# One-layer hybrid decoder step on one core: two-operand work of the FFN moved from GpSimd to VectorE

## The chip, the core and the metric

The kernel runs on one core of one Trainium2 chip. The metric is device time in microseconds (us) of one execution. Engines are named as the profile names them: PE is TensorE's matmul row and PEld its weight loads, DVE is VectorE, ACT is ScalarE, POOL is GpSimd, SP is SyncE, which here issues all large DMAs.

## The reference

The reference computes one decoder layer for 512 prompt tokens and 8 x 8 sample tokens (576 token columns in the kernel). What matters here is its second half, the output projection, the ConvGLU and the last norm:

```python
x = x + jnp.concatenate([ya, yb, yc], axis=-1) @ w_out        # 2048 x 2048
h2 = rms_norm(x, norm2)
gc, new_ffn = causal_dwconv(h2 @ w_gate, ffn_buf, ffn_conv_w) # 2048 x 5504, 3 taps
x = x + (jax.nn.silu(gc) * (h2 @ w_up)) @ w_down              # 5504 x 2048
y = rms_norm(x, final_norm)
```

All data is float32.

## The kernel before

Activations lie transposed, channels on the 128 partitions and 576 token columns along the free side, split into two halves of 288 columns (`HALF`). A float32 product is made of three matmuls in a reduced float32 form: every operand is split into a high part (ACT, a copy with rounding) and a low part (DVE, source minus high part). For weights that is `split_w` (lines 827 and 828), for activations `split_sb` (lines 174 and 175).

The program is written as one straight line. A scheduler puts the instructions in order for each engine, and each engine then works its list strictly in that order; an instruction waits on semaphores for its inputs and for buffers. The stages of the profiled execution are: input projection and attention (to about 970 us), output projection (`project(w_out, ...)`, to about 1155), a first change of stage (to about 1200) in which the second norm is prepared, gate and up products (to about 2160), a second change of stage (to about 2240), down products in four chunks (to about 2690), and a tail.

Gate, up and down use one level of Strassen's method in Winograd's form, `strassen` (line 839 is its matmul). One call loads four weight tiles b11, b12, b22, b21, forms combinations of them in place, splits seven tiles, and runs seven products. Each product is 24 matmuls of 128 x 288 in gate and up (8 blocks of 128 rows, three matmuls each, weight tiles 128 x 1024) and 15 in down (5 blocks, tiles 128 x 640). The products run into three PSUM tiles, `a`, `b` and `e`, in the order p1, p5, u2, p2, u3, p53, c21. Several products add into the same PSUM tile, so an eviction has to be read before the next product on that tile starts: u2 is read out of `a` before the product of u3 adds to it, u3 before that of c21. Between the two there is always one product on another tile.

Gate and up calls alternate: a gate call makes two gate tiles (`combine` with `gate_first` and `gate_second`, which multiply by the norm's factor `rstd2`), then an up call finishes the pair before it (`times`). The convolution and the activation of a gate pair (`conv_silu`: ACT, four DVE operations of 592 columns, ACT, two POOL multiplications) are put into the up call that follows it, one step after each eviction.

In the first change of stage, `own_halves` and `mixed_halves` split the last activations, and the rows `ssb` of sums of squares become `rstd2` (`rsqrt`: DVE line 184, ACT line 185, then DVE again). In the down stage `first_halves` prepares the activations of chunk 0 and `act_halves` those of chunks 1 to 3, during the chunk before, as far as the 28 slots for activations go; a chunk has 18. `add_to` adds each product to two of the 16 residual tiles.

The four weight combinations of one call are in lines 870 (DVE), 874 (POOL), 875 (DVE) and 880 (POOL).

Of the kernel before, what the change touches and what calls it, by code (L numbers as in the profile page):

```python
# [10 lines left out]
F32 = mybir.dt.float32  # L11
# [69 lines left out]
def decoder_step(ctx: ExitStack, tc, I, O):  # L81
# [778 lines left out]
    def strassen(load, X, evac, split, n, early=None):  # L860
# [13 lines left out]
        nc.gpsimd.tensor_sub(b12, b22, b12)  # L874
# [29 lines left out]
    for m in range(KD):  # L904
# [16 lines left out]
        else:  # L921
# [6 lines left out]
            nc.gpsimd.tensor_add(s12[:, :HALF], v0[:, HALF:], v[:, HALF:])  # L928
            nc.gpsimd.tensor_sub(s12[:, HALF:], s12[:, :HALF], v0[:, :HALF])
# [69 lines left out]
    def combine(sink0, sink1, sink2, sink3):  # L999
# [3 lines left out]
        def evac(place, ps):  # L1003
# [9 lines left out]
            elif place == "u3":  # L1013
                nc.scalar.copy(s2[:, HALF:], ps)
                nc.gpsimd.tensor_add(s1[:, HALF:], s2[:, HALF:], s1[:, HALF:])
# [10 lines left out]
    def gate_first(e, eng):  # L1026
        return lambda src: eng.tensor_mul(e[:, 2:2 + HALF], src, r0)

    def gate_second(e, eng):
        def sink(src):  # L1030
            eng.tensor_mul(e[:, 2 + HALF:2 + NP], src[:, :NPH], r1[:, :NPH])
            eng.tensor_mul(ext_a(e)[:, :, 2:10], src[:, NPH:].rearrange("p (b t) -> p b t", b=NB),
                           r1[:, NPH:].rearrange("p (b t) -> p b t", b=NB))
        return sink

    def conv_silu(ff, e, nst, f, nf):
# [55 lines left out]
    for nf in GROUPS:  # L1092
# [287 lines left out]
```

## Time and profile before

| | |
|---|---|
| median of 3 runs | 2761.15 us (2757.96 to 2763.15) |
| the profiled execution's own time | 2761.27 us |
| its span in the profile | 2759.5 us |
| PE busy | 2582.1 us (94% of the span) |
| PEld busy | 2514.7 us (91%) |
| DVE busy | 1952.0 us (71%) |
| POOL busy | 1273.4 us (46%) |
| ACT busy | 981.0 us (36%) |
| mean granted TensorE clock | 0.972 of full speed |

Matmuls are pipelined and their ends are modelled, so PE counts as busy while matmuls follow one another, and PE's work in a stretch is best read from the number of matmuls in it. An instruction that is held up while it runs shows as a longer duration, not as idle time. Idle time ahead of an instruction stands in brackets in a timeline, with the instruction that ended it. Line numbers are those of the kernel before; the changed kernel is 11 lines shorter, so its later lines have numbers smaller by 1 to 11.

### The profile page before, as it was taken

The numbers are of one execution on the slowest core, as the hardware profiler recorded it, in microseconds if no ns is written. First come the engines' busy times: TensorE is split into PE (matmuls) and PEld (weight loads), VectorE is DVE, ScalarE is ACT, GpSimd is POOL, SyncE is SP. The second block draws the span as 40 slices with busy tenths as digits, with TensorE's granted clock in tenths as the row PEclk, the third lists the DMA queues.
The fourth block names the chain that finished last, engine by engine and source line by source line (L and its number), as shares of the span: only waits on it lengthen the run. The fifth ranks groups of instructions, "written<-read, shape, count | busy, mean of one in ns | idle before, by whom it ended". The sixth has DMA issues, their size and how long they took to land.

```text
span 2759.5 us, 48907 instructions
## 1 busy us (share of the span) xinstructions
PE 2582.1 (94%) x19844; PEld 2514.7 (91%) x19844; DVE 1952.0 (71%) x2231; ACT 981.0 (36%) x1498; POOL 1273.4 (46%) x932
## 2 busy tenths in 40 slices
PE   8998998997988999889999999999999798989997
PEld 8988998997988999889999999999999698989997
DVE  5236467467477633597878788888878889898985
ACT  6121221221211333344444444444444444443445
POOL 0027027125248011465656555665656645454544
PEclk9999999999999999989999999999999899999999
DMA  8345368268466775335555555545555745444534
GB/s 254 112 105 146 88 178 216 73 174 218 124 172 170 240 243 184 123 102 161 163 159 158 165 157 155 166 155 163 160 158 166 251 150 153 147 147 146 158 101 143
DMA packets 602804, 441.60 MB, mean 160 GB/s; under 512 B 22167, under 2 KB 568642, under 8 KB 596178
## 3 DMA queue, kind: packets, MB, share of 16 engines
q1 hardware_dynamic: 602578, 438.47, 53.4%
q8 instruction: 156, 2.56, 0.4%
q14 instruction: 70, 0.57, 0.1%
HBM read 398.17 MB, written 127.50 MB: 190 GB/s over the span
## 4 chain that ended last, share of the span: by engine, by line
PE 50%; DVE 19%; issue 11%; DMA 8%; POOL 5%; ACT 4%; SPq 2%; ACTq 0%; DVEq 0%; POOLq 0%
PE acc L839 16%; PE acc L155 6%; PE acc L156 6%; PE acc L157 6%; DVE wl L828 5%; PE pt L839 4%; PE s L839 4%; PE ps L839 4%; ACT wh L827 4%; DVE av L516 2%; DMA ek<-in_cache_kv_w_dram 2%; DVE wr L870 2%; DMA out_dram<-in_cache_kv_w_dram 2%; POOL eq L433 2%; POOL prod L433 2%
## 5 line engine op out<-in xcount | busy, mean ns | idle before, releaser
L828 DVE TENSOR_TENSOR wl<-wr,wh 128x640 fp32r<-128x640 f32 (+1 forms) x396 | 559.0, 1420 | 201.0 <-ACT wh L827 197.0
L155 PE MATMUL acc<-xs,wh 128*128 128x288 f32 x2208 | 664.3, 302 | 2.9 <-DVE t L700 1.5
L157 PE MATMUL acc<-xs,wl 128*128 128x288 f32 x2208 | 659.9, 299 | 4.6 <-DVE wl L142 4.6
L156 PE MATMUL acc<-xs,wh 128*128 128x288 f32 x2208 | 661.4, 300 | 0.0
L827 ACT ACTIVATE wh<-wr 128x640 fp32r<-128x640 f32 (+1 forms) x396 | 343.6, 876 | 695.4 <-DVE wr L875 282.2
L155 PEld LDWEIGHTS acc<-xs,wh 128*128 128x128 f32 x2208 | 420.8, 191 | 10.4 <-issue 4.6
L157 PEld LDWEIGHTS acc<-xs,wl 128*128 128x128 f32 x2208 | 422.9, 192 | 7.3 <-DVE wl L142 5.3
L839 PE MATMUL acc<-xs,wh 128*128 128x288 f32 x2048 | 419.2, 297 | 7.4 <-DVE wk L1235 3.4
L156 PEld LDWEIGHTS acc<-xs,wh 128*128 128x128 f32 x2208 | 421.4, 191 | 2.9 <-issue 2.5
L141 ACT ACTIVATE wh<-wr 128x1024 fp32r<-128x1024 f32 (+1 forms) x150 | 155.6, 1038 | 563.8 <-PE acc L156 512.2
L839 PEld LDWEIGHTS acc<-xs,wh 128*128 128x128 f32 x2048 | 330.6, 190 | 9.1 <-DVE wk L1235 3.9
L839 PE MATMUL acc<-xs,wl 128*128 128x288 f32 x1024 | 303.8, 297 | 1.3 <-DVE wl L828 1.2
L142 DVE TENSOR_TENSOR wl<-wr,wh 128x1024 fp32r<-128x1024 f32 (+1 forms) x150 | 213.7, 1425 | 121.5 <-ACT wh L141 115.0
L839 PE MATMUL acc<-x,wh 128*128 128x288 f32 x1196 | 247.4, 298 | 29.9 <-ACT wk L1005 15.7
L880 POOL TENSOR_TENSOR wx<-wx,wr 128x1024 f32<-128x1024 f32 x43 | 132.7, 3085 | 197.5 <-DVE wl L828 197.5
L839 PEld LDWEIGHTS acc<-x,wh 128*128 128x128 f32 x1196 | 192.5, 190 | 30.8 <-ACT wk L1005 16.0
L433 POOL TENSOR_TENSOR ek<-qb,ek 128x1024 f32<-128x1024 f32 x32 | 79.4, 2486 | 268.6 <-DMA qb<-qd 177.8
L839 PEld LDWEIGHTS acc<-xs,wl 128*128 128x128 f32 x1024 | 194.2, 190 | 2.3 <-DVE wl L828 2.0
L839 PE MATMUL acc<-x,wl 128*128 128x288 f32 x598 | 177.5, 297 | 5.8 <-DVE wl L828 5.5
L828 DVE TENSOR_TENSOR wl<-wx,wh 128x1024 fp32r<-128x1024 f32 x129 | 166.0, 1297 | 12.4 <-ACT wh L827 12.2
L839 PE MATMUL s<-xs,wh 128*128 128x288 f32 x660 | 138.8, 300 | 17.5 <-ACT wh L827 15.5
L827 ACT ACTIVATE wh<-wx 128x1024 fp32r<-128x1024 f32 x129 | 135.6, 1051 | 35.7 <-PE ps L839 35.2
(411 smaller groups left out, 5534.5 us busy)
## 6 DMA issues: line engine op xcount, KB each, us to landing
out_dram<-in_cache_kv_w_dram SPq DMA_DIRECT2D x320, 204.0 KB
wr<-in_w_in_dram SPq DMA_DIRECT2D x110, 512.0 KB
wr<-in_w_down_dram SPq DMA_DIRECT2D x128, 320.0 KB
ek<-in_cache_kv_w_dram SPq DMA_DIRECT2D x52, 512.0 KB
ev<-in_cache_kv_w_dram SPq DMA_DIRECT2D x52, 512.0 KB
wx<-in_w_gate_dram SPq DMA_DIRECT2D x43, 512.0 KB
wr<-in_w_gate_dram SPq DMA_DIRECT2D x43, 512.0 KB
wr<-in_w_up_dram SPq DMA_DIRECT2D x43, 512.0 KB
```

Of the source, the lines that this page charges most:

```text
L141: nc.scalar.activation(hi[:, :n], dst, AF.Copy)
L142: low.tensor_sub(lo[:, :n], dst, hi[:, :n].bitcast(F32))
L155: nc.tensor.matmul(o, wh, xh, start=first, stop=False)
L156: nc.tensor.matmul(o, wh, xl, start=False, stop=False)
L157: nc.tensor.matmul(o, wl, xh, start=False, stop=last)
L433: nc.gpsimd.tensor_mul(pv_, qv, keys)
L516: nc.vector.scalar_tensor_tensor(av[:, t, :], v[:, t, :], w, av[:, t, :], op0=ALU.mult, op1=ALU.add)
L827: nc.scalar.activation(hi[:, :n], src, AF.Copy)
L828: nc.vector.tensor_sub(lo[:, :n], src, hi[:, :n].bitcast(F32))
L839: nc.tensor.matmul(o, a[:, ws], b, start=first and k == 0 and i == 0, stop=k == n - 1 and i == 2, skip_group_check=True)
L870: nc.vector.tensor_sub(b11, b12, b11)
L880: nc.gpsimd.tensor_sub(b21, b21, b11)
```

## The change

All two-operand work of the FFN stages that POOL did goes to DVE, except the fourth weight combination of each call (`b21 - b11`, line 880), the sums of squares (`ssq`), and the first two sums of `act_halves` (`s12`). The subtraction b22 - b12 (line 874) goes to DVE; so do the sums of `s12` in the output projection, the odd half of `mixed_halves` and of its counterpart in `first_halves`, the sums of `first_halves`, the last subtraction of `act_halves`, the multiplications by `rstd2` in `gate_first`, `gate_second` and `conv_silu`, and all of `times`. Two kinds of eviction change as well: u3 of gate and up, and p5 and u2 of down, went from PSUM to SBUF by an ACT copy and were then added by POOL; now one DVE addition reads PSUM and adds. The last tile's up product, which a POOL copy moved, is moved by ACT.

```diff
@@ strassen
         b21 = load(1, 0)
-        nc.gpsimd.tensor_sub(b12, b22, b12)
+        nc.vector.tensor_sub(b12, b22, b12)
         nc.vector.tensor_sub(b11, b22, b11)
...
@@ output projection
-            nc.gpsimd.tensor_add(s12[:, :HALF], v0[:, HALF:], v[:, HALF:])
-            nc.gpsimd.tensor_sub(s12[:, HALF:], s12[:, :HALF], v0[:, :HALF])
+            nc.vector.tensor_add(s12[:, :HALF], v0[:, HALF:], v[:, HALF:])
+            nc.vector.tensor_sub(s12[:, HALF:], s12[:, :HALF], v0[:, :HALF])
@@ mixed_halves
-            (nc.gpsimd if i % 2 else nc.vector).tensor_sub(vv, vv, s2)
+            nc.vector.tensor_sub(vv, vv, s2)
@@ combine
             elif place == "u3":
-                nc.scalar.copy(s2[:, HALF:], ps)
-                nc.gpsimd.tensor_add(s1[:, HALF:], s2[:, HALF:], s1[:, HALF:])
+                nc.vector.tensor_add(s1[:, HALF:], ps, s1[:, HALF:])
                 sink3(s1[:, HALF:])
@@ conv_silu
-            nc.gpsimd.tensor_mul(prm(s), c[:, 0:NP], prm(rstd2))
-            nc.gpsimd.tensor_mul(smp_bt(s), ...
+            nc.vector.tensor_mul(prm(s), c[:, 0:NP], prm(rstd2))
+            nc.vector.tensor_mul(smp_bt(s), ...
@@ up_pair
-                 combine(times(g1, 0, nc.vector), times(g2, 0, nc.vector), times(g1, 1, nc.vector),
-                         times(g2, 1, nc.gpsimd)), split_w, 8)
+                 combine(times(g1, 0), times(g2, 0), times(g1, 1), times(g2, 1)), split_w, 8)
@@ gate pair
-                         combine(gate_first(e1, nc.gpsimd), gate_first(e2, nc.gpsimd), gate_second(e1, nc.vector),
-                                 gate_second(e2, nc.gpsimd)), split_w, 8)
+                         combine(gate_first(e1), gate_first(e2), gate_second(e1), gate_second(e2)), split_w, 8)
@@ first_halves
-            nc.gpsimd.tensor_add(ae[:, HALF:], ae[:, HALF:], ao[:, HALF:])
-            nc.gpsimd.tensor_sub(ae[:, :HALF], ae[:, HALF:], ae[:, :HALF])
+            nc.vector.tensor_add(ae[:, HALF:], ae[:, HALF:], ao[:, HALF:])
+            nc.vector.tensor_sub(ae[:, :HALF], ae[:, HALF:], ae[:, :HALF])
...
-                    (nc.gpsimd if i % 2 else nc.vector).tensor_sub(halves(src), halves(src), s2)
+                    nc.vector.tensor_sub(halves(src), halves(src), s2)
@@ act_halves
-            nc.gpsimd.tensor_sub(halves(ao), halves(ao), s2)
+            nc.vector.tensor_sub(halves(ao), halves(ao), s2)
@@ add_to
-            if place == "p5":
-                nc.scalar.copy(sn[:, :HALF], ps)
-                nc.gpsimd.tensor_add(x22, x22, sn[:, :HALF])
-            elif place == "u2":
-                nc.scalar.copy(sn[:, HALF:], ps)
-                nc.gpsimd.tensor_add(x12, x12, sn[:, HALF:])
-            else:
-                x = {"p1": x11, "p2": x11, "u3": x22, "p53": x12, "c21": x21}[place]
-                nc.vector.tensor_add(x, ps, x)
+            x = {"p1": x11, "p2": x11, "p5": x22, "u3": x22, "u2": x12, "p53": x12, "c21": x21}[place]
+            nc.vector.tensor_add(x, ps, x)
```

The scheduler orders the changed program anew. First, DVE's list where an up call follows a gate call, from the first weight combination of the up call (line 870) to the first convolution operation. `wr` and `wx` are weight tiles, `wl` low parts, `pt`, `s` and `acc` PSUM tiles, `wk_11734` is `rstd2`. Before:

```order
L870 TENSOR_TENSOR wr_13872<-wx_13874,wr_13872 128x1024
L1018 TENSOR_TENSOR wk_13632<-pt_13635,wk_13632 128x288
L828 TENSOR_TENSOR wl_13911<-wr_13872,wh_13910 128x1024
L1031 TENSOR_TENSOR wk_13625<-acc_13633,wk_11734 128x224
L1032 TENSOR_TENSOR wk_13625<-acc_13633,wk_11734 128x8x8
L875 TENSOR_TENSOR wr_13872<-wr_13876,wr_13872 128x1024
L828 TENSOR_TENSOR wl_13950<-wr_13872,wh_13949 128x1024
L828 TENSOR_TENSOR wl_13985<-wx_13945,wh_13984 128x1024
L1046 SCALAR_TENSOR_TENSOR wk_13863<-wk_13625,fcw,wk_13863 128x592
```

The same place in the changed kernel:

```order
L870 TENSOR_TENSOR wr_13864<-wx_13866,wr_13864 128x1024
L1017 TENSOR_TENSOR wk_13625<-pt_13628,wk_13625 128x288
L874 TENSOR_TENSOR wx_13866<-wr_13868,wx_13866 128x1024
L1026 TENSOR_TENSOR wk_13621<-wk_13625,wk_11734 128x288
L828 TENSOR_TENSOR wl_13903<-wr_13864,wh_13902 128x1024
L1030 TENSOR_TENSOR wk_13618<-acc_13626,wk_11734 128x224
L1031 TENSOR_TENSOR wk_13618<-acc_13626,wk_11734 128x8x8
L875 TENSOR_TENSOR wr_13864<-wr_13868,wr_13864 128x1024
L828 TENSOR_TENSOR wl_13942<-wr_13864,wh_13941 128x1024
L828 TENSOR_TENSOR wl_13977<-wx_13937,wh_13976 128x1024
L1045 SCALAR_TENSOR_TENSOR wk_13855<-wk_13618,fcw,wk_13855 128x592
```

Line 874 and one multiplication now stand between line 870 and the split of its result; everything else keeps its place. Second, DVE's list in the first change of stage, up to line 184, the start of `rsqrt`. Before (`L950` is the subtraction of `mixed_halves`, `L175` the split of an activation):

```order
L175 TENSOR_TENSOR xs_11863<-wk_10707,xs_11863 128x576
L175 TENSOR_TENSOR xs_11896<-wk_10957,xs_11896 128x576
L175 TENSOR_TENSOR xs_11899<-wk_11209,xs_11899 128x576
L950 TENSOR_TENSOR wk_10957<-wk_10957,ev_10965 128x576
L175 TENSOR_TENSOR xs_11902<-wk_11460,xs_11902 128x576
L175 TENSOR_TENSOR xs_11905<-wk_11711,xs_11905 128x576
L175 TENSOR_TENSOR xs_11944<-wk_9953,xs_11944 128x576
L950 TENSOR_TENSOR wk_10957<-wk_10957,ev_10965 128x576
L175 TENSOR_TENSOR xs_11949<-wk_10204,xs_11949 128x576
L950 TENSOR_TENSOR wk_11460<-wk_11460,xs_11468 128x576
L175 TENSOR_TENSOR xs_11954<-wk_10455,xs_11954 128x576
L184 TENSOR_SCALAR wk_11735<-wk_11727 128x576
```

In the changed kernel, the last 12 instructions up to the same point:

```order
L950 TENSOR_TENSOR wk_10707<-wk_10707,ev_10714 128x576
L175 TENSOR_TENSOR xs_11902<-wk_11460,xs_11902 128x576
L950 TENSOR_TENSOR wk_10957<-wk_10957,ev_10965 128x576
L175 TENSOR_TENSOR xs_11905<-wk_11711,xs_11905 128x576
L950 TENSOR_TENSOR wk_11209<-wk_11209,xs_11216 128x576
L175 TENSOR_TENSOR xs_11944<-wk_9953,xs_11944 128x576
L950 TENSOR_TENSOR wk_10707<-wk_10707,ev_10714 128x576
L175 TENSOR_TENSOR xs_11949<-wk_10204,xs_11949 128x576
L950 TENSOR_TENSOR wk_11460<-wk_11460,xs_11468 128x576
L175 TENSOR_TENSOR xs_11954<-wk_10455,xs_11954 128x576
L950 TENSOR_TENSOR wk_10957<-wk_10957,ev_10965 128x576
L184 TENSOR_SCALAR wk_11735<-wk_11727 128x576
```

Of the 11 instructions ahead of line 184 three were subtractions; in the changed kernel six are. On ACT at this place, as a piece of the difference:

```order
 L185 ACTIVATE wk_11736<-wk_11735 128x576
-L174 ACTIVATE xs_12000<-wk_11209 128x576
 L1005 COPY wk_11813<-acc_11815 128x288
 L1007 COPY wk_11813<-s_11817 128x288
+L174 ACTIVATE xs_12000<-wk_11209 128x576
 L174 ACTIVATE xs_12005<-wk_11460 128x576
```

The eviction of the first gate product (line 1005) moved ahead of one activation split. Third, DVE's list in the down stage, from the end of one call into the next. Before:

```order
L828 TENSOR_TENSOR wl_24452<-wr_24445,wh_24451 128x640
L870 TENSOR_TENSOR wr_24445<-wr_24447,wr_24445 128x640
L1235 TENSOR_TENSOR wk_22704<-s_24283,wk_22704 128x288
L828 TENSOR_TENSOR wl_24473<-wr_24445,wh_24472 128x640
L1235 TENSOR_TENSOR wk_22702<-acc_24281,wk_22702 128x288
L875 TENSOR_TENSOR wr_24445<-wr_24449,wr_24445 128x640
L1235 TENSOR_TENSOR wk_22706<-acc_24442,wk_22706 128x288
L828 TENSOR_TENSOR wl_24498<-wr_24445,wh_24497 128x640
L828 TENSOR_TENSOR wl_24519<-wr_24493,wh_24518 128x640
L828 TENSOR_TENSOR wl_24540<-wr_24447,wh_24539 128x640
L828 TENSOR_TENSOR wl_24560<-wr_24449,wh_24559 128x640
L1235 TENSOR_TENSOR wk_22706<-ps_24443,wk_22706 128x288
```

The same place in the changed kernel:

```order
L870 TENSOR_TENSOR wr_24371<-wr_24373,wr_24371 128x640
L1224 TENSOR_TENSOR wk_22661<-s_24212,wk_22661 128x288
L874 TENSOR_TENSOR wr_24373<-wr_24375,wr_24373 128x640
L828 TENSOR_TENSOR wl_24399<-wr_24371,wh_24398 128x640
L1224 TENSOR_TENSOR wk_22659<-acc_24210,wk_22659 128x288
L875 TENSOR_TENSOR wr_24371<-wr_24375,wr_24371 128x640
L1224 TENSOR_TENSOR wk_22663<-acc_24368,wk_22663 128x288
L828 TENSOR_TENSOR wl_24423<-wr_24371,wh_24422 128x640
L828 TENSOR_TENSOR wl_24443<-wr_24418,wh_24442 128x640
L1224 TENSOR_TENSOR wk_22665<-pt_24370,wk_22665 128x288
L828 TENSOR_TENSOR wl_24464<-wr_24373,wh_24463 128x640
L1224 TENSOR_TENSOR wk_22665<-acc_24368,wk_22665 128x288
```

Line 874 stands ahead of a split here too, and the evictions of p5 (from `pt`) and u2 (from `acc`) now stand between the splits, so DVE waits for a product there before it goes on.

## Rows read from the trace of the kernel before

**Rows 1.** Windows: stretch, length, busy us (count) of PE, PEld, DVE, ACT, POOL; clock.
```profile
1020.00:1120.00 100.00, 100.00 (x752) 100.00 (x752) 33.15 (x32) 30.54 (x40) 21.25 (x16) 1.00 0.58 183
1160.00:1200.00 40.00, 19.25 (x115) 17.75 (x116) 35.26 (x32) 17.33 (x28) 22.45 (x22) 0.70 0.27 82
1200.00:2140.00 940.00, 922.84 (x6853) 909.22 (x6852) 761.42 (x635) 397.42 (x548) 571.16 (x471) 1.00 0.51 159
2160.00:2240.00 80.00, 55.77 (x357) 52.66 (x356) 70.94 (x81) 36.08 (x63) 50.28 (x39) 0.83 0.76 241
...
2240.00:2690.00 450.00, 423.12 (x3055) 415.41 (x3054) 394.50 (x460) 191.82 (x313) 220.84 (x152) 0.97 0.48 144
2300.00:2360.00 60.00, 49.93 (x324) 47.41 (x323) 58.93 (x64) 27.74 (x48) 40.79 (x28) 0.91 0.49 146
```
**Rows 2.** Waits of PE and PEld, 1190 to 2140: total us, times, longest.
```profile
PEld ps L839 <- ACT wh L827: 8.9, 39, 0.3
...
PE s L839 <- ACT wh L827: 15.5, 20, 0.9
```
**Rows 3.** Timeline of one up call, from 1601: start, us, engine, line.
```profile
1602.55 4.48 DVE L1046 SCALAR_TENSOR_TENSOR wk<-wk,fcw,wk 128x592 f32<-128x592 f32 x3
1602.72 2.93 POOL L880 TENSOR_TENSOR wx<-wx,wr 128x1024 f32<-128x1024 f32 x1 [3.47 <-DVE wl L828]
...
1607.06 0.70 ACT L1054 ACTIVATE wk<-wk 128x592 f32<-128x592 f32 x1 [2.99 <-DVE wk L1046]
```
**Rows 4.** Timeline where an up call follows a gate call, from 1636.
```profile
1636.36 1.56 POOL L1015 TENSOR_TENSOR wk<-wk,wk 128x288 f32<-128x288 f32 x1 [3.37 <-ACT wk L1014]
...
1637.29 1.71 DVE L870 TENSOR_TENSOR wr<-wx,wr 128x1024 f32<-128x1024 f32 x1
...
1640.04 2.40 POOL L874 TENSOR_TENSOR wx<-wr,wx 128x1024 f32<-128x1024 f32 x1
1640.22 3.29 DVE L828 TENSOR_TENSOR wl<-wr,wh 128x1024 fp32r<-128x1024 f32 x1 [0.84 <-ACT wh L827]
```
**Rows 5.** Durations in ns, min/median/max, of single DVE lines over the whole span.
```profile
L828 DVE TENSOR_TENSOR wl<-wx,wh x129: 1210/1219/3449, 1160.8 to 2164.6; 128x1024 fp32r<-128x1024 f32 x129
...
L175 DVE TENSOR_TENSOR xs<-s,xs x9: 741/753/1221, 2209.9 to 2579.1; 128x576 fp32r<-128x576 f32 x9
...
L1235 DVE TENSOR_TENSOR wk<-acc,wk x96: 442/445/459, 2195.1 to 2695.5; 128x288 f32<-128x288 f32 x96
...
L1046 DVE SCALAR_TENSOR_TENSOR wk<-wk,fcw,wk x86: 820/1336/2995, 1210.0 to 2156.7; 128x592 f32<-128x592 f32 x86
```
**Rows 6.** Timeline of the first change of stage.
```profile
1161.09 1.77 POOL L928 TENSOR_TENSOR wk<-wk,wk 128x288 f32<-128x288 f32 x1
...
1164.50 5.40 DVE L175 TENSOR_TENSOR xs<-wk,xs 128x576 fp32r<-128x576 f32 x4 [2.29 <-ACT xs L174]
...
1181.18 0.45 DVE L184 TENSOR_SCALAR wk<-wk 128x576 f32<-128x576 f32 x1
...
1182.83 0.38 ACT L1005 COPY wk<-acc 128x288 f32<-128x288 f32 x1
...
1183.26 0.84 PE L839 MATMUL acc<-x,wh 128*128 128x288 f32 x2 [15.67 <-ACT wk L1005]
```
**Rows 7.** Timeline of the second change of stage, DVE.
```profile
2163.77 0.45 DVE L1011 TENSOR_TENSOR wk<-ps,wk 128x288 f32<-128x288 f32 x1
...
2188.84 0.81 DVE L828 TENSOR_TENSOR wl<-wr,wh 128x640 fp32r<-128x640 f32 x1
```
**Rows 8.** Groups of instructions by shape, 2300 to 2360: busy us, mean ns.
```profile
L828 DVE TENSOR_TENSOR wl<-wr,wh 128x640 fp32r<-128x640 f32 x21 | 28.3, 1368 | 0.7 <-ACT wh L827 0.7
...
L1201 POOL TENSOR_TENSOR s<-s,al 128x288 f32<-128x288 f32 x5 | 6.3, 1266 | 0.2
L1200 POOL TENSOR_TENSOR s<-al,al 128x288 f32<-128x288 f32 x5 | 6.3, 1263 | 2.5 <-DMA al<-act 1.5 <-DVE wk L1235 1.0
L880 POOL TENSOR_TENSOR wr<-wr,wr 128x640 f32<-128x640 f32 x3 | 6.3, 2104 | 0.0
```

More of the change, by code (lines that the diff above doesn't have):

```diff
@@ L1024, in combine, with gate_first, gate_second @@
         return evac
-    def gate_first(e, eng):
-        return lambda src: eng.tensor_mul(e[:, 2:2 + HALF], src, r0)
-    def gate_second(e, eng):
+    def gate_first(e):
+        return lambda src: nc.vector.tensor_mul(e[:, 2:2 + HALF], src, r0)
+    def gate_second(e):
         def sink(src):
-            eng.tensor_mul(e[:, 2 + HALF:2 + NP], src[:, :NPH], r1[:, :NPH])
-            eng.tensor_mul(ext_a(e)[:, :, 2:10], src[:, NPH:].rearrange("p (b t) -> p b t", b=NB),
-                           r1[:, NPH:].rearrange("p (b t) -> p b t", b=NB))
+            nc.vector.tensor_mul(e[:, 2 + HALF:2 + NP], src[:, :NPH], r1[:, :NPH])
+            nc.vector.tensor_mul(ext_a(e)[:, :, 2:10], src[:, NPH:].rearrange("p (b t) -> p b t", b=NB),
+                                 r1[:, NPH:].rearrange("p (b t) -> p b t", b=NB))
         return sink
@@ L1056, in fourth @@
         def fourth():
-            nc.gpsimd.tensor_mul(prm(s), c[:, 0:NP], prm(rstd2))
-            nc.gpsimd.tensor_mul(smp_bt(s), c[:, NP + 2:NP + 82].rearrange("p (b x) -> p b x", x=10)[:, :, 0:8],
+            nc.vector.tensor_mul(prm(s), c[:, 0:NP], prm(rstd2))
+            nc.vector.tensor_mul(smp_bt(s), c[:, NP + 2:NP + 82].rearrange("p (b x) -> p b x", x=10)[:, :, 0:8],
                                  smp_bt(rstd2))
@@ L1067, in new_e, with times @@
         return e
-    def times(s, h, eng):
+    def times(s, h):
         sh = s[:, h * HALF:(h + 1) * HALF]
-        return lambda src: eng.tensor_mul(sh, src, sh)
+        return lambda src: nc.vector.tensor_mul(sh, src, sh)
     def state_out(nst, f0, nf):
@@ L1117, in decoder_step @@
                 strassen(loader([(w_g, ff * P), (w_u, ff * P)]), h2,
-                         combine(gate_first(e1, nc.gpsimd), lambda src: nc.gpsimd.tensor_copy(u[:, :HALF], src),
-                                 gate_second(e1, nc.vector), lambda src: nc.gpsimd.tensor_copy(u[:, HALF:], src)),
+                         combine(gate_first(e1), lambda src: nc.scalar.copy(u[:, :HALF], src),
+                                 gate_second(e1), lambda src: nc.scalar.copy(u[:, HALF:], src)),
                          split_w, 8)
@@ L1221, in add_to @@
     def add_to(xa, xb):
-        sn = fp.tile([P, TOK], F32, tag="sn", bufs=2, name=nm("sn"))
         x11, x21, x12, x22 = xa[:, :HALF], xa[:, HALF:], xb[:, :HALF], xb[:, HALF:]
         def evac(place, ps):
-            if place == "p5":
-                nc.scalar.copy(sn[:, :HALF], ps)
-                nc.gpsimd.tensor_add(x22, x22, sn[:, :HALF])
-            elif place == "u2":
-                nc.scalar.copy(sn[:, HALF:], ps)
-                nc.gpsimd.tensor_add(x12, x12, sn[:, HALF:])
-            else:
-                x = {"p1": x11, "p2": x11, "u3": x22, "p53": x12, "c21": x21}[place]
-                nc.vector.tensor_add(x, ps, x)
+            x = {"p1": x11, "p2": x11, "p5": x22, "u3": x22, "u2": x12, "p53": x12, "c21": x21}[place]
+            nc.vector.tensor_add(x, ps, x)
         return evac
```

## The prediction

> **What bounds the kernel now.** I first read the windows, by stage. A stretch in which PE runs at its full rate, inside the output projection, has 752 matmuls in 100 us, 7.52 per us. Divide the matmuls of each later stretch by that rate, and what is left of its length is time that PE lost [rows 1]: 115/7.52 = 15.3 of 40 us in the first change of stage (24.7 lost), 6853/7.52 = 911.3 of 940 in gate and up (28.7 lost), 357/7.52 = 47.5 of 80 in the second change (32.5 lost), 3055/7.52 = 406.2 of 450 in down (43.8 lost). That is 129.7 us, and it bounds what any change to DVE and POOL can bring: below 2761 - 130 = 2631 us PE itself ends the kernel. PE's 94% busy hides this, since a waiting or slowly clocked PE often shows as busy.
>
> Next the waits of PE in gate and up. Two kinds make up most of the 28.7 us: one matmul per pair waits for ACT's split (20 times, 15.5 us), and the weight loads of `ps` wait a little in every call (39 times, 8.9 us) [rows 2]. Both waits end at ACT, but ACT is idle most of the time, so the question is what holds ACT up. The timeline shows it. In the up call three convolution operations take 4.48 us on DVE, while POOL's line 880 runs from 1602.72 to 1605.65 [rows 3]; undisturbed, one takes 0.82 us [rows 5], so three take 2.5. ACT's Silu has waited 2.99 us for them when it starts at 1607.06 [rows 3], and in ACT's list the split that PE wants stands right behind it.
>
> So operations of DVE and POOL hold each other up. The plainest case: a split of 1024 columns that takes 1.21 us undisturbed [rows 5] starts at 1640.22, just after POOL's line 874 at 1640.04, and takes 3.29 us: POOL's end at 1642.44 plus about 1.1 [rows 4]. Line 870 next to POOL's line 1015 takes 1.71 [rows 4]. Additions that read PSUM do not suffer: 96 of them lie between 442 and 459 ns, with POOL busy beside many of them [rows 5].
>
> **What the change costs and brings, part by part.** The sum is made on the profiled execution's own 2761.27 us, which stands 0.1 us above the median.
>
> *Gate and up.* Per pair of calls (44.7 us of matmuls: 336/7.52) DVE gains two subtractions of line 874 (1.2 us each, as line 828), four multiplications of `conv_silu` (two of 512 columns, between 0.45 for 288 and 0.75 for 576, say 0.7; two of 64, at most 0.45), two evictions of u3 (0.45) and five more multiplications of at most 288 columns (0.45 each, with a short piece beside one): 2.4 + 2.3 + 0.9 + 2.7 = 8.3 us. What it had is 761.4 us in 940, or 36.2 in a pair of 44.7 [rows 1], and that contains the hold-ups. Nine instructions of 1024 columns a call at 1.21 (21.8), four of 592 at 0.82 (3.3) and some ten short ones (4.4) are 29.5, so hold-ups take 6.7. In the changed kernel only line 880 and a few tiny copies stay on POOL. If their hold-up is a full 2.4 us per line 880, DVE has 29.5 + 8.3 + 4.8 = 42.6 of 44.7 us to do; with none, 37.8. It fits, but not by much.
>
> Does the chain to PE get shorter? At the start of an up call DVE now works line 870, an eviction, line 874, a multiplication, the split. From 1637.29 that is 1.21 + 0.45 + 1.21 + 0.46 + 1.21 = 4.5 us, to 1641.8; before, the split ended at 1640.22 + 3.29 = 1643.5. Everything behind it in DVE's list (line 875, two splits, the convolution) moves up by the 1.7 us, and little is added ahead of the third convolution operation. Line 880 still falls on the convolution, so I count 1.0 of the 1.7 as kept: more than the 0.78 us that the matmul waits in one pair (15.5/20). The order of PE's list is the same there. I take all 15.5 us and 6.5 of the 8.9: **-22**, with bounds of -28 (all that was lost) and +12 (below).
>
> *First change of stage.* PE waits 15.67 us for the eviction at 1182.83, which stands behind `rsqrt` on ACT, which waits for line 184 at 1181.18 [rows 6]. Ahead of that, DVE's splits take 5.40 for four, 1.35 each, against 0.75 undisturbed [rows 5]. From the first of them to line 184 it is 16.7 us now; in the new list it is 15 instructions of at most 0.75, 11.3, and line 880 may hold one up for 2.4. That brings 3.0 to 5.4. The two sums on POOL ahead of the first split (1.77 for the first [rows 6], 2.6 for both) become two DVE additions of 0.45: 1.7. The eviction itself moves ahead of one ACT split, 0.6. Sum 5.3 to 7.7; for splits of mixed halves that could become the next to be late I take **-7** with bounds of -3 and -13.
>
> *Second change of stage.* From the eviction at 2163.77 to the end of the first down split at 2189.65 DVE works 25.9 us [rows 7]. The new list has 37 instructions between: 11 of 576 columns (8.3), 24 short ones (10.8), two splits (2.0), together 21.1, and POOL's two sums of `act_halves` may cost up to 2.5. That is **-5** at most and 2.3 with the hold-ups; the next two splits gain again by line 874's leaving POOL, so I keep -5, with bounds of 0 (the loads of `act` and of weights come no earlier) and -11.
>
> *Down.* In the middle of a chunk PE runs at its rate. The loss is at the ends of chunks, where `act_halves` goes on beside the calls. There DVE is the bound: 58.93 busy of 60 us [rows 1]. Its 64 instructions at undisturbed durations are 28 of 640 columns (0.81, so 22.7), 15 of 576 (11.3), 21 short ones (9.5), 43.4; hold-ups take the other 15.5, which is 38% of POOL's 40.8. Line 828 alone lost 21 x (1.37 - 0.81) = 11.8 [rows 8]. After the change POOL keeps 6.3 + 6.3 + 6.3 = 18.9 of its 40.8 [rows 8], at 38% a hold-up of 7.2. DVE gains four of line 874, five subtractions of 576 columns and six evictions: 3.2 + 3.8 + 2.7 = 9.7. New demand: 43.4 + 9.7 + 7.2 = 60.3, against 58.9. So here the change takes from POOL about what it puts on DVE; what it gains is a shorter chain through one engine fewer, perhaps 1 to 2 us at each of three boundaries. I take **-4** for the stage; the bounds are -20 (half of what was lost) and +20, the latter with hold-ups for all of POOL's 18.9, which adds 11.7 to each of two long boundaries and less to the last. The Trainium skill ("SBUF — State Buffer", section "Who interferes with whom") says that of a VectorE instruction with two SBUF inputs and a GpSimd instruction that reads SBUF, the one that comes second is blocked for the whole of the other. By that rule the kept 18.9 us would all be lost if POOL always came first, and this term would be about +20 instead of -4; the rows bear the rule out for a single pair of instructions, but over the window DVE lost 38% of POOL's time.
>
> *Elsewhere.* The two sums per pair of output tiles that move to DVE lie in a stage where DVE is busy 33% and PE runs without a gap [rows 1]: nothing. Without that cover they would cost 8 x 0.9 us. No DMA changes; loads of weights wait for line 880 to free a buffer, and it comes no later.
>
> Sum: -22 - 7 - 5 - 4 = -38, so 2761.3 - 38 = **2723 us**.
>
> **The rivals.** *DVE becomes the bound in down.* Evictions of p5 and u2 now stand in DVE's list between splits, and DVE was already full at chunk boundaries. Then down is +20 while the rest holds at -30 or so: about 2750. For it: 58.93 of 60. Against it: mid-chunk DVE has nine splits and combinations plus seven evictions, 8.1 + 0.8 + 3.2 = 12.1 us in 14 us of matmuls (105/7.52). The Trainium skill ("Perfetto Trace Analysis", section "Optimizing Scalar/DVE Operations") speaks for this rival, since it lets work go to GpSimd where VectorE is saturated.
>
> *Slower: a late eviction stops PE in every gate and up call.* The eviction of u3 was ACT's, and ACT was seldom late; now it is DVE's line 1014, behind a split and a multiplication. The product of c21 adds to the same PSUM tile, so PE stops when that eviction comes later than one product, 24/7.52 = 3.2 us, after u3's end. By the sum above DVE has 2 to 7 us of slack in a pair. If line 880 and waits on PE eat 4 more, each of 43 calls loses 1 to 2 us: +43 to +86 in place of -22, with the other terms some 2790. That upper end is not my bound of +12, which is 0.3 us a call.
>
> *No change.* If PE's 0.78 us wait is only moved to the next split that stands behind a Silu, gate and up give 0 and the rest of the gains and losses cancel: 2757 to 2767.
>
> *More than forecast.* If DVE's hold-ups at chunk boundaries vanish, down gives -20 and the total is 2700 or less.
>
> **How the numbers follow.** Forecast (2700 to 2740): 0.65. DVE bound in down (2740 to 2755): 0.16. Slower: 0.09. No change: 0.05. More: 0.05. 0.2% is 5.5 us, about what a measurement of this kernel can tell from none. Faster is the forecast, the first rival and the last, 0.86; same 0.05; slower 0.09. The range 2698 to 2753 holds the forecast and most of the first rival, 0.8.
>
> **What would show it.** In the changed profile: no DVE row of 1024 columns above 1.3 us except beside line 880; PE's wait for ACT in up calls gone from 15.5 us to under 4; 7.4 matmuls per us or more in gate and up; line 184 five to eight us earlier relative to the last matmul of the output projection; DVE still near 60 of 60 us at chunk boundaries. I am wrong if PE waits for line 1014 or 1224 in steady calls, or if gate and up keep their rate of 7.29.

## The result, and the profile after

The changed kernel takes **2712.09 us** (median of 4 runs, 2709.63 to 2712.75) against 2760.43 us for the kernel before on the same chip, a ratio of 0.9819 (95% interval 0.9806 to 0.9831). The forecast was 2723, with a range of 2698 to 2753. The profiled execution spans 2710.8 us against 2759.5, 48.7 less. The first part of the page of after (busy us, share, instructions):

```profile
span 2710.8 us, 48680 instructions
...
PE 2564.9 (95%) x19844; PEld 2512.2 (93%) x19844; DVE 1923.0 (71%) x2656; ACT 960.8 (35%) x1393; POOL 673.4 (25%) x505
```

POOL lost 600 us of its 1273.4, and DVE, which took that work over, is busy 29 us less than before. That alone says that DVE's busy time before contained much waiting.

To see where the 48.7 us came from, I take five landmarks that both traces have: the last matmul of the output projection (line 157), the first and the last DVE eviction of p2 in gate and up (line 1011), and the first and the last DVE addition from `acc` in down (line 1235 before, 1224 after). The rows of the lines over the whole span, each with count, ns min/median/max, first and last start; before:

```profile
L1011 DVE TENSOR_TENSOR wk<-ps,wk x43: 442/446/458, 1193.0 to 2163.8; 128x288 f32<-128x288 f32 x43
```

and after:

```profile
L157 PE MATMUL acc<-xs,wl x2208: 289/295/610, 14.2 to 1151.4; 128*128 128x288 f32 x184
...
L1011 DVE TENSOR_TENSOR wk<-ps,wk x43: 443/457/458, 1184.2 to 2121.7; 128x288 f32<-128x288 f32 x43
...
L1224 DVE TENSOR_TENSOR wk<-acc,wk x128: 443/457/460, 2146.3 to 2646.8; 128x288 f32<-128x288 f32 x128
```

The lengths between the landmarks, for the two kernels and all experiments (us; the tail, from the last landmark to the end of the span, is 64.0 to 64.2 in all of them):

| kernel | start to last matmul of w_out | first change | gate and up | second change | down |
|---|---|---|---|---|---|
| before | 1153.3 | 39.7 | 970.8 | 31.3 | 500.4 |
| after | 1151.4 | 32.8 | 937.5 | 24.6 | 500.5 |
| after_again | 1154.4 | 32.8 | 936.3 | 24.8 | 499.3 |
| only_874 | 1154.0 | 38.6 | 937.5 | 30.6 | 497.2 |
| only_evict | 1153.6 | 39.7 | 942.1 | 30.8 | 492.5 |
| only_rest | 1150.7 | 33.9 | 965.2 | 24.1 | 498.6 |
| down_before | 1155.2 | 32.8 | 937.1 | 32.3 | 497.7 |
| dummy_sub | 1152.1 | 34.5 | 963.2 | 23.9 | 494.8 |
| dummy_copy | 1151.0 | 33.7 | 939.2 | 24.3 | 496.1 |
| late_rsqrt | 1154.7 | 30.2 | 938.1 | 24.8 | 496.5 |
| dve_880 | 1154.3 | 31.8 | 934.8 | 24.2 | 494.4 |
| down_evict | 1153.6 | 32.8 | 937.4 | 24.9 | 494.4 |
| down_evict_again | 1155.4 | 32.8 | 937.5 | 24.8 | 494.9 |
| best | 1160.8 | 30.2 | 938.8 | 26.0 | 495.5 |

So the 48.7 us are 1.9 in the stages ahead (less than that column's own scatter), 6.9 in the first change of stage, **33.3 in gate and up**, 6.7 in the second change and nothing in down. The table also tells how well each column can be read. The first column scatters by 10 us over kernels that hardly differ there. Down scatters by 5.7 us (494.8 to 500.5) over five kernels whose down stage has the same source (after, after_again, dummy_sub, dummy_copy, late_rsqrt). In the first four of these PE, DVE, ACT and POOL even work the same instructions there in the same order, and nearly all of the difference lies in two distances between p2's evictions of successive calls: from the first to the second call of chunk 1 (19.5, 17.8, 17.7 and 17.7 us) and into the first call of chunk 3 (23.4, 21.8, 19.6 and 20.9). What sets these two is open. Gate and up, and the first change, repeat within 1.2 us.

Windows of after, columns as in [rows 1]: gate and up, and the start of a chunk boundary, at the same phase as 2300 to 2360 before:

```profile
1191.00:2099.00 908.00, 907.32 (x6850) 906.65 (x6849) 743.23 (x903) 394.31 (x507) 196.80 (x203) 1.00 0.53 164
...
2250.00:2310.00 60.00, 49.91 (x317) 46.65 (x316) 51.36 (x76) 25.89 (x41) 16.57 (x13) 0.89 0.52 156
```

In gate and up 6850 matmuls now take 908 us, 7.54 per us, which is PE's full rate; before it was 7.29 [rows 1]. At the boundary PE does as few matmuls as before (317 against 324), but DVE is busy 51.36 of 60 us, no longer 58.93. The waits of the weight loads in gate and up (1200 to 2100: total us, times, longest), first before, then after:

```profile
PEld s L839 <- ACT wh L827: 19.7, 19, 1.1
PEld ps L839 <- ACT wh L827: 8.8, 38, 0.3
```

```profile
PEld acc L839 <- DVE wl L828: 0.6, 1, 0.6
PEld ps L839 <- ACT wh L827: 0.5, 1, 0.5
```

In these rows the 28.5 us of waits for ACT became 0.5, and the longest wait left is 0.6 us for a DVE split. The same stretch of an up call as in [rows 3, 4], in the timeline of after:

```profile
1525.24 1.23 DVE L870 TENSOR_TENSOR wr<-wx,wr 128x1024 f32<-128x1024 f32 x1
...
1526.75 1.22 DVE L874 TENSOR_TENSOR wx<-wr,wx 128x1024 f32<-128x1024 f32 x1
1527.88 0.46 DVE L1026 TENSOR_TENSOR wk<-wk,wk 128x288 f32<-128x288 f32 x1
1528.25 1.22 DVE L828 TENSOR_TENSOR wl<-wr,wh 128x1024 fp32r<-128x1024 f32 x1
...
1534.53 4.47 DVE L1045 SCALAR_TENSOR_TENSOR wk<-wk,fcw,wk 128x592 f32<-128x592 f32 x3
1534.74 2.88 POOL L880 TENSOR_TENSOR wx<-wx,wr 128x1024 f32<-128x1024 f32 x1 [3.53 <-issue]
...
1539.03 0.70 ACT L1053 ACTIVATE wk<-wk 128x592 f32<-128x592 f32 x1 [2.17 <-DVE wk L1045]
1539.63 1.04 ACT L827 ACTIVATE wh<-wr 128x1024 fp32r<-128x1024 f32 x1
```

The split that line 874 held up takes 1.22 us instead of 3.29. The convolution beside line 880 still takes 4.47, as in [rows 3]; yet the Silu waits 2.17 us instead of 2.99, and ACT's split that PE needs (the last row) is in time.

### The profile page after: what moved, and what is told of

Its sections match the earlier page's. It is cut to its first block, busy times and chain, and to the rows that moved or that the text cites. A ratio compares the mean times of both kernels' runs of the same rounds, so it can differ in the third digit from the quotient of the medians.

```text
span 2710.8 us, 48680 instructions
## 1 busy us (share of the span) xinstructions
PE 2564.9 (95%) x19844; PEld 2512.2 (93%) x19844; DVE 1923.0 (71%) x2656; ACT 960.8 (35%) x1393; POOL 673.4 (25%) x505
## 4 chain that ended last, share of the span: by engine, by line
PE 72%; DVE 10%; DMA 6%; issue 5%; POOL 5%; ACT 1%; SPq 1%; DVEq 0%; POOLq 0%; ACTq 0%
PE acc L839 27%; PE ps L839 7%; PE acc L155 7%; PE pt L839 7%; PE acc L156 7%; PE s L839 7%; PE acc L157 7%; DMA ek<-in_cache_kv_w_dram 3%; POOL eq L433 2%; POOL prod L433 2%; DVE av L516 2%; DVE wl L142 1%; DVE xs L175 1%; DVE wl L828 1%; DMA al<-act 1%
## 5 line engine op out<-in xcount | busy, mean ns | idle before, releaser
L828 DVE TENSOR_TENSOR wl<-wr,wh 128x640 fp32r<-128x640 f32 (+1 forms) x396 | 413.3, 1051 | 105.4 <-ACT wh L827 102.9
L880 POOL TENSOR_TENSOR wx<-wx,wr 128x1024 f32<-128x1024 f32 x43 | 117.3, 2728 | 443.7 <-DVE wl L828 371.1
L828 DVE TENSOR_TENSOR wl<-wx,wh 128x1024 fp32r<-128x1024 f32 x129 | 167.3, 1298 | 40.1 <-ACT wh L827 38.6
```

What stands on the lines that cost most here:

```text
L828: nc.vector.tensor_sub(lo[:, :n], src, hi[:, :n].bitcast(F32))
L880: nc.gpsimd.tensor_sub(b21, b21, b11)
```

## Experiments

There are two theories at the start. **Hold-up**: DVE and POOL instructions with operands in SBUF stop each other, and PE waits in the end for a DVE split that POOL held up. **Chain**: the results themselves came late, because evictions and products passed through ACT and the slower POOL. Three runs make one part of the change each.

**only_874**, the kernel before with one line:

```diff
-        nc.gpsimd.tensor_sub(b12, b22, b12)
+        nc.vector.tensor_sub(b12, b22, b12)
```

> The kernel before with one line changed: the subtraction b22 - b12 (line 874) on VectorE, everything else as before. Hold-up theory (operations of POOL and DVE with SBUF operands stop each other, and the splits of DVE are what PE waits for in the end): the split beside line 874 falls from 3.3 us to 1.2, gate and up gain 15 to 28 us of the 32 that the whole change brought there, the first change of stage nothing, the time is 2732 to 2745. Chain theory (the gain comes from evictions and products that pass through one engine fewer): gate and up gain at most 5, time 2755 to 2760.

Measured: 2724.77 us, ratio 0.9859 (0.9844 to 0.9873). One line brings all 33.3 us of gate and up, and 1.1 in the first change. The time is below the ranges of both theories.

**only_evict**, the kernel before with the evictions alone:

```diff
-                nc.scalar.copy(s2[:, HALF:], ps)
-                nc.gpsimd.tensor_add(s1[:, HALF:], s2[:, HALF:], s1[:, HALF:])
+                nc.vector.tensor_add(s1[:, HALF:], ps, s1[:, HALF:])
...
+            x = {"p1": x11, "p2": x11, "p5": x22, "u3": x22, "u2": x12, "p53": x12, "c21": x21}[place]
```

> The kernel before with the evictions of u3 (gate, up) and of p5 and u2 (down) by one DVE addition from PSUM, everything else as before, so ACT has fewer copies and POOL fewer additions. Hold-up theory: gate and up gain 2 to 8 us, since only 1.6 us of POOL work a call goes; down is within 5 us of before; time 2750 to 2760. Chain theory: gate and up gain 15 to 30, time 2730 to 2745.

Measured: 2727.69 us, ratio 0.987 (0.9856 to 0.9885). This also brings 28.7 of the 33.3 us, as the chain theory had it, though the time is again below both ranges. The timeline of an up call shows why both do, though:

```profile
1488.31 1.06 ACT L827 ACTIVATE wh<-wr 128x1024 fp32r<-128x1024 f32 x1 [2.31 <-PE acc L839]
...
1492.12 2.40 POOL L874 TENSOR_TENSOR wx<-wr,wx 128x1024 f32<-128x1024 f32 x1
1493.19 2.41 DVE L828 TENSOR_TENSOR wl<-wr,wh 128x1024 fp32r<-128x1024 f32 x1 [0.84 <-ACT wh L827]
...
1505.94 1.04 ACT L827 ACTIVATE wh<-wr 128x1024 fp32r<-128x1024 f32 x1
```

The split is still held until POOL's line 874 ends, but line 874 starts 1.07 us ahead of it, not 0.18 as in [rows 4], because the addition of line 1015 (1.56 us) is no longer queued ahead of it on POOL. So the hold-up ends earlier. Both runs shorten the same place.

**only_rest**, the changed kernel without these two parts (line 874 and the three evictions as before):

```diff
-        nc.vector.tensor_sub(b12, b22, b12)
+        nc.gpsimd.tensor_sub(b12, b22, b12)
...
```

> The changed kernel with line 874 back on GpSimd and the three evictions back on ACT and GpSimd: only the multiplications, the sums of the output projection, mixed_halves, first_halves and the last subtraction of act_halves are moved. Hold-up theory: first change of stage 8 to 9 us earlier and second 5 to 7 as in the changed kernel, gate and up gain 3 to 15 through line 1046 and its neighbours; time 2735 to 2745. Chain theory: the same at the changes of stage and nothing in gate and up: 2745. If the parts act one by one, the gains of this run and of the two others add up to the 48 us of the whole change.

Measured: 2742.15 us, ratio 0.9918 (0.9904 to 0.9933). The gains of the three runs, from their ratios, are 39, 36 and 23 us, 98 together, about twice the 50 of the whole change (ratio 0.9819). In gate and up only_rest brings 5.6 us: its weight loads wait for `ps` no longer (0.6 us), but for `s` as long as before (20.0 us, 19 times). The parts don't add up, because several of them remove the same wait.

How late may that split be? I take the chain of one up call from the ACT split that has waited for PE (the first row above, tied to PE's own pace) to the start of the split that PE waits for behind the Silu (the last row): 1505.94 - 1488.31 = 17.63. The median over the up calls of each trace that begin with such a wait (13 to 24 of them):

| kernel | chain, us | PE's weight loads wait for `s` |
|---|---|---|
| before | 18.92 | 19.7 us, 19 times |
| only_rest | 18.83 | 20.0 us, 19 times |
| dummy_sub (below) | 18.46 | 15.6 us, 19 times |
| only_evict | 17.65 | 1.1 us, once |
| dummy_copy (below) | 17.61 | 0.5 us, once |
| only_874 | 17.57 | never |
| after | 16.77 | never |

PE's matmul waited up to 0.89 us in such a call before, which puts the limit near 18.92 - 0.89 = 18.03; in dummy_sub it waited 0.63 with a chain of 18.46, which puts it near 17.8. So the limit lies between 17.7, where only_evict has one such wait in all, and 18.0. Whatever moves the chain below it brings the whole of this wait, and what moves it further brings nothing. That is a third, **threshold** theory, which the next runs test.

**dummy_sub** adds a GpSimd instruction whose result nobody reads to the changed kernel, **dummy_copy** one with a single operand:

```diff
+        ws1 = split(w, b11)
+        if n == 8:
+            nc.gpsimd.tensor_sub(scr[0], ws1[0][:, :w].bitcast(F32), ws1[0][:, :w].bitcast(F32))
-        product(e, split(w, b11), c["s1"], True)
+        product(e, ws1, c["s1"], True)
...
+    scr = [wx.tile([P, 1024], F32, tag="scr", bufs=1, name="scr")]
```

(in dummy_copy `nc.gpsimd.tensor_copy(scr[0], ws1[0][:, :w].bitcast(F32))`)

> The changed kernel with one GpSimd instruction more in each gate and up call: the subtraction of two SBUF tiles, 128 x 1024, into a scratch tile that nobody reads, at the place where line 874 stood in time (it needs the high part of the split of line 870's result). No other instruction needs it, so only a hold-up can make the kernel slower. Hold-up theory: the split beside it takes 2.5 to 3.6 us instead of 1.22, DVE's list is 1 to 2 us later in every call, and the waits of PE come back: gate and up 15 to 45 us longer, time 2727 to 2757. Chain theory (only the result of line 874 came too late): no change, 2708 to 2716.

> The same with a GpSimd copy of one SBUF tile of 128 x 1024 in place of the subtraction of two. If any GpSimd instruction that reads SBUF holds DVE up for its whole length: as much longer as with the subtraction, in proportion to its own duration. If only instructions with two SBUF operands do: 2708 to 2716, with the splits at 1.22 us.

Measured: dummy_sub 2739.62 us, ratio 0.9922 (0.9904 to 0.9941), dummy_copy 2711.63 us, ratio 0.9832 (0.9804 to 0.9859). The timeline of dummy_sub where the new instruction runs:

```profile
1537.99 1.22 DVE L877 TENSOR_TENSOR wx<-wr,wx 128x1024 f32<-128x1024 f32 x1
1539.03 1.93 POOL L873 TENSOR_TENSOR scr<-wh 128x1024 f32<-128x1024 f32 x1 [2.53 <-ACT wh L827]
1539.13 2.15 DVE L1030 TENSOR_TENSOR wk<-wk,wk 128x288 f32<-128x288 f32 x1
1541.20 1.21 DVE L828 TENSOR_TENSOR wl<-wr,wh 128x1024 fp32r<-128x1024 f32 x1
```

and of dummy_copy:

```profile
1528.83 1.09 POOL L873 COPY scr<-wh 128x1024 f32<-128x1024 f32 x1 [2.50 <-ACT wh L827]
1528.94 1.29 DVE L1030 TENSOR_TENSOR wk<-wk,wk 128x288 f32<-128x288 f32 x1
```

A multiplication of 288 columns that takes 0.46 us takes 2.15, up to POOL's end at 1540.96 plus 0.3. An instruction whose result nobody reads made gate and up 25.7 us longer (963.2), and the wait for `s` came back (15.6 us, 19 times), that for `ps` in part (6.3 us, 20 times). The trace names no instruction that waited for it, nor for the buffer that it reads. That shows the hold-up, apart from any chain of results. My expectation named the wrong victim: it was the multiplication ahead of the split, while the split itself took 1.21. The copy of one operand holds DVE up for its whole length as well; the idea that only POOL instructions with two operands do so falls. It costs no time because it is short: 0.83 us later, the chain is still below the limit. The Trainium skill ("SBUF — State Buffer", section "Who interferes with whom") has the rule so: a VectorE instruction with two SBUF inputs contends with a GpSimd instruction that reads SBUF; the trace agrees, with 2.15 and 1.29 us for the 0.46.

**dve_880**, the changed kernel with the last combination on VectorE too:

```diff
-        nc.gpsimd.tensor_sub(b21, b21, b11)
+        nc.vector.tensor_sub(b21, b21, b11)
```

> The changed kernel with the last weight combination (line 880) on VectorE too, in all calls. Threshold theory (PE only waits when the split of b22 comes later than some 18 us behind the start of its chain; the changed kernel is already earlier): the three convolution operations take 2.5 us instead of 4.5, the split comes another 1 to 2 us earlier, and gate and up take exactly as long as in the changed kernel; 2708 to 2716 with what down adds or gives. If gate and up gain in proportion to the hold-up removed: 2685 to 2700.

Measured: 2706.93 us, ratio 0.9804 (0.979 to 0.9818), beside after_again with 0.9815 (0.9801 to 0.9828). The convolution over the whole span (ns min/median/max), in dve_880 and in the changed kernel:

```profile
L1045 DVE SCALAR_TENSOR_TENSOR wk<-wk,fcw,wk x86: 823/828/835, 1197.4 to 2115.3; 128x592 f32<-128x592 f32 x86
```

```profile
L1045 DVE SCALAR_TENSOR_TENSOR wk<-wk,fcw,wk x86: 819/827/2991, 1198.0 to 2115.1; 128x592 f32<-128x592 f32 x86
```

The hold-up is gone altogether (at most 835 ns instead of 2991), and gate and up take 934.8 us, 1.5 to 2.7 less than the changed kernel's two profiles. The scheduler has also put the split that PE needs ahead of the Silu in ACT's list:

```profile
1538.15 1.06 ACT L827 ACTIVATE wh<-wr 128x1024 fp32r<-128x1024 f32 x1 [2.00 <-PE acc L839]
...
1539.40 1.29 ACT L1053 ACTIVATE wk<-wk 128x592 f32<-128x592 f32 x2
```

This split starts 15.99 us after the start of its chain (1522.16), 0.8 less than in the changed kernel, and it waits for PE, not PE for it. To start it still earlier was worth next to nothing, as the threshold theory has it. It is not a test of the full hold-up, though: DVE's three convolution operations end only 1.0 us earlier after the start of the first (3.46 us against 4.47), since the subtraction now takes its 1.22 us between them.

**down_before**, the changed kernel with the down stage and its preparation as before:

```diff
-        nc.vector.tensor_sub(b12, b22, b12)
+        (nc.vector if n == 8 else nc.gpsimd).tensor_sub(b12, b22, b12)
-            nc.vector.tensor_add(ae[:, HALF:], ae[:, HALF:], ao[:, HALF:])
+            nc.gpsimd.tensor_add(ae[:, HALF:], ae[:, HALF:], ao[:, HALF:])
...
-            nc.vector.tensor_sub(halves(ao), halves(ao), s2)
+            nc.gpsimd.tensor_sub(halves(ao), halves(ao), s2)
```

> The changed kernel with the whole down stage as before (line 874 of down calls, evictions of p5 and u2, first_halves and the last subtraction of act_halves back on GpSimd). Balance theory (in down the change takes from POOL about what it puts on DVE): the stage as a whole takes as long as in the changed kernel, but the boundary before chunk 2 is 5 to 6 us longer and that before chunk 3 as much shorter; the second change of stage gives back 5 to 7; time 2715 to 2722. DVE-bound theory (the moved evictions cost the down stage time that other parts hide): time 2695 to 2707.

Measured: 2718.93 us, ratio 0.9835 (0.9818 to 0.9851). The second change gives back 7.7 us (32.3), and down is 497.7, within the scatter, so balance holds for the stage. Its boundaries moved less than expected. Over three distances between p2's evictions, the one before chunk 2 is 2.7 us longer than in the changed kernel (60.0 against 57.3), not 5 to 6, and the one before chunk 3 is 2.5 to 4.1 shorter, where the changed kernel itself scatters by as much.

**down_evict** keeps only the evictions and `first_halves` in down:

```diff
-        nc.vector.tensor_sub(b12, b22, b12)
+        (nc.vector if n == 8 else nc.gpsimd).tensor_sub(b12, b22, b12)
-            nc.vector.tensor_sub(halves(ao), halves(ao), s2)
+            nc.gpsimd.tensor_sub(halves(ao), halves(ao), s2)
```

> The changed kernel with two parts of the down stage back on GpSimd: line 874 of the down calls and the last subtraction of act_halves; the evictions of p5 and u2 and first_halves stay on VectorE. In the run with only the evictions the down stage was 8 us shorter than before, in the changed kernel 0.6. If the parts act here as they did there, the time is 2712 - 7 = 2705 and the wait at the boundary before chunk 3 is gone. If the gain there came from what else was as before (first_halves, the phase of the calls), 2710 to 2716.

> The kernel of down_evict once more beside the changed kernel. Its down stage was 7.8 us shorter there by the matmuls' positions, and the stages ahead of the edits some 3 us longer, which I take for scatter. If so: 4 to 9 us below the changed kernel on the same chip. If the stages ahead really are longer: 0 to 3 below.

> The changed kernel once more, on the chip of the three runs beside it, so that differences of a few us can be read: 2708 to 2716 by all theories.

Measured: down_evict 2710.19 us (ratio 0.9814), down_evict_again 2707.86 (ratio 0.9803, 0.9789 to 0.9817), after_again 2711.18 (ratio 0.9815). Down takes 494.4 and 494.9 us, 4 to 6 less than the two profiles of the changed kernel, but the same as dummy_sub (494.8), whose down code is the changed kernel's. The distance into chunk 3 is 19.0 and 19.1 us, against 19.6 to 23.4 with the changed kernel's down code. The times of down_evict_again and after_again differ by 3 us with overlapping intervals. Whether this version is faster is not settled.

**late_rsqrt** and **best** try the wait that is left in the first change of stage; best has this edit on top of down_evict's:

```diff
-    rsqrt(work, ssb, rstd2)
+    first_own = later[0]
+    later[0] = lambda: (rsqrt(work, ssb, rstd2), first_own())
```

> The changed kernel with the second norm's rsqrt written behind the first gate product's eviction, so that ACT's list has this eviction ahead of line 185. It tests whether PE's 14.0 us wait in the first change of stage is that place in ACT's list. If so, the wait shrinks to a few us and the time is 2698 to 2706. If the splits behind it on DVE are as late, PE waits for them instead: 2708 to 2714.

> The kernel of down_evict with the rsqrt behind the first gate eviction as in late_rsqrt. If both gains are real and separate: 6 to 11 us below the changed kernel on the same chip, 2700 to 2706. If the late rsqrt only moves the wait: the same as down_evict.

Measured: late_rsqrt 2707.24 us, ratio 0.9801 (0.9783 to 0.982); best 2707.5 us, ratio 0.9811 (0.9794 to 0.9828). The first change is 2.6 us shorter (30.2), not 14. The eviction now comes at 1166.60, and PE waits for others (1150 to 1200):

```profile
PE acc L839 <- DVE xs L175: 4.6, 1, 4.6
PE ps L981 <- ACT wk L968: 3.2, 1, 3.2
```

The activation splits on DVE are next in line. No version is shown to beat the changed kernel.

## Why the prediction was right, and where it was off

**Gate and up: the mechanism right, the size too small.** I took -22 with a lower bound of -28; it was -33.3. The place was right: DVE's list from line 870 on came earlier by 16.56 - 14.39 = 2.2 us (medians of the chain from line 870's start to ACT's split), where I had 1.7 before deductions. The term that was mis-sized is the price of the wait: I priced it by the idle time of matmuls, 15.5 us [rows 2], and took 6.5 of the 8.9 of the weight loads of `ps`. The weight loads of `s` wait longer than the matmuls behind them, 1.1 us against 0.9, and over the whole stage (1193 to 2164) the waits of PEld are 20.4 us for `s`, 8.9 for `ps` and 1.1 for `pt`, 30.4 in all. My sum left PEld's row of `s` out. The other 3 us are spread over gaps that no row names. My bound of -28 divided a stretch that left out the first and last calls. The rival "slower" did not come: the waits of PE and PEld in this stage name line 1014 nowhere.

My reason for keeping only a part, that line 880 still falls on the convolution, was true (4.47 us) and without effect: with the threshold it was enough to be 0.9 to 1.2 us earlier. DVE is busy 743.23 of 908 us, which is 36.6 in a pair of 44.7, where I had 37.8 to 42.6: the sum of single durations is too high, as the down stage shows below.

**First change: -7 forecast, -6.9 measured, in part by luck.** Rows of after:

```profile
1158.88 4.93 DVE L175 TENSOR_TENSOR xs<-wk,xs 128x576 fp32r<-128x576 f32 x4
...
1171.09 0.45 DVE L184 TENSOR_SCALAR wk<-wk 128x576 f32<-128x576 f32 x1
1171.20 0.68 ACT L174 ACTIVATE xs<-wk 128x576 fp32r<-128x576 f32 x1 [1.99 <-DVE wk L950]
1171.90 1.28 ACT L185 ACT_TABLE_LOAD   x1
1173.19 0.68 ACT L185 ACTIVATE wk<-wk 128x576 f32<-128x576 f32 x1
1173.78 0.38 ACT L1005 COPY wk<-acc 128x288 f32<-128x288 f32 x1
...
1174.21 0.85 PE L839 MATMUL acc<-x,wh 128*128 128x288 f32 x2 [13.99 <-ACT wk L1005]
```

Line 184 starts 19.7 us after the last matmul of w_out, and before 27.9 [rows 6]: 8.2 earlier, just above the 5 to 8. Of these, 4.5 lie between the first of the activation splits and line 184 (12.2 us instead of 16.7), as forecast (3.0 to 5.4), and 3.7 ahead of the first split, where I had 1.7. The eviction comes only 7.1 us earlier. I had it gain 0.6 on line 184; it lost 1.0, because line 185 now stands on ACT behind a split that waited 1.99 us for a subtraction of line 950 and behind a table load of 1.28 us. So two misses cancel in the sum. The wait for line 1005 itself is only 1.7 us shorter, 13.99 instead of 15.67, because PE comes to it 5.5 us earlier: PE's wait for POOL's list (line 963), 3.5 us before, is gone:

```profile
PE ps L967 <- POOL wk L963: 3.5, 1, 3.5
```

Only_rest has nearly all of it (33.9), as the sum said: it is `mixed_halves` and the two sums.

**Second change: -5 forecast, -6.7 measured**, all of it in kernels whose `first_halves` is on DVE, none in the others (30.6 to 32.3). In after DVE takes 19.9 us from the eviction of p2 to the end of the first down split, where it took 25.9 [rows 7] and I had 21.1:

```profile
2121.70 0.46 DVE L1011 TENSOR_TENSOR wk<-ps,wk 128x288 f32<-128x288 f32 x1
...
2140.82 0.81 DVE L828 TENSOR_TENSOR wl<-wr,wh 128x640 fp32r<-128x640 f32 x1
```

Line 874's leaving POOL gave nothing there (only_874 30.6).

**Down: -4 forecast, 0 in this pair of profiles; with a scatter of 5.7 us a gain of 4 is neither shown nor excluded. The account of the boundary was wrong.** I held DVE to be the bound at chunk boundaries, with a new demand of 60.3 us in 60. It is busy 51.36, and the boundary is no shorter. The demand was too high for two reasons. I added up single durations, and those of instructions that follow one another overlap: the 76 in this window add up to 56.6 us while DVE is busy 51.36. And the hold-ups are small: line 828 takes 892 ns there, against 1368 before [rows 8] and 0.81 us undisturbed. So a full DVE is not what bounds the boundary. Over the stage (2146 to 2650, before 2195 to 2700) PE's waits are 33.5 us, and 33.0 before; DVE instructions end 20.9 of them instead of 25.6, ACT's 12.6 instead of 7.4. What the change took from one it gave to the other. The timeline of after shows what was late at one of PE's longest waits there:

```profile
2271.44 1.62 POOL L1197 TENSOR_TENSOR s<-al,al 128x288 f32<-128x288 f32 x1 [6.44 <-DVE ev L175]
...
2273.13 0.79 POOL L1198 TENSOR_TENSOR s<-s,al 128x288 f32<-128x288 f32 x1
2273.96 0.68 ACT L174 ACTIVATE xs<-s 128x576 fp32r<-128x576 f32 x1 [2.89 <-POOL s L1198]
...
2275.12 0.72 ACT L827 ACTIVATE wh<-wr 128x640 fp32r<-128x640 f32 x1
...
2275.89 0.85 PE L839 MATMUL pt<-ek,wh 128*128 128x288 f32 x2 [2.35 <-ACT wh L827]
```

ACT's weight split stands in its list behind two activation splits, the first of which waits for POOL's sums of `act_halves`. That this order of work, more than any engine's time, sets the boundary is argued from the rows; `act_halves`' sums on DVE were not tried. The waits of PE for line 1224 are 6.0 us over the stage, 5.7 for line 1235 before. The rival of a DVE-bound down stage (+20) did not come. In the middle of a chunk DVE is busy 11.6 us of a call of 13.9, near my 12.1 (whose nine splits and combinations are ten in the kernel).

**Elsewhere**: the sums of the output projection cost nothing that shows, as forecast; the first column scatters by 10 us with and without them.

Of the marks that I named, those on DVE's rows, on the waits in up calls and on the rate held, and line 184 came 0.2 us beyond its mark. DVE at 60 of 60 us at chunk boundaries did not hold.

## What to carry to other kernels

A wait that repeats once per call can be a threshold, as it was here: find how late the instruction is against the limit. The first edit that removes that much then gets the whole gain, while further ones get none, so gains of parts don't add. Price such a wait by the weight loads' row and by the stage's matmul rate, not by the idle time of matmuls alone. To see whether an engine is full, do not add up single durations where its instructions overlap. An engine that reads busy may be held up: if undisturbed durations from other places add up to much less than its busy time, moving work to it from the engine that holds it up can make it less busy.

## What the runs showed of the hardware

POOL work that no one waited for cost 25.7 us of gate and up, though it was only 1.93 us a call, and a one-operand copy (1.09 us) stopped a DVE multiplication as fully as a two-operand subtraction did.

A long wait of PE costs more than its length. Windows of after (columns as in [rows 1]), ahead of the end of the 13.99 us wait, right behind it, and later:

```profile
1160.00:1174.00 14.00, 0.23 (x2) 0.00 (x0) 14.00 (x19) 8.12 (x14) 1.92 (x3) 0.61 0.19 57
...
1175.00:1179.00 4.00, 4.00 (x19) 4.00 (x18) 4.00 (x4) 1.41 (x3) 0.00 (x0) 0.50 0.94 324
1182.00:1190.00 8.00, 8.00 (x63) 8.00 (x62) 6.65 (x11) 2.17 (x3) 0.52 (x3) 1.00 0.48 137
```

The granted clock fell during the wait and stood at 0.50, the lower level of 1.2 GHz, when PE went on: 19 matmuls in 4 us, 4.8 per us, and at 1.00 afterwards 63 in 8, 7.9 per us (such short windows count the matmuls at both edges, so both rates are a little high). PE read 100% busy in both.
